# Expert weights built from one-hot products in the rounded format, with the weight's rounded part and rest side by side

## The chip, the cores and the metric

The kernel runs on one core of a Trainium2 chip. The time is device microseconds of one execution. TensorE is called PE in the views (its weight loads PEld), VectorE is DVE, ScalarE is ACT, GpSimd is POOL and SyncE, which here only starts transfers, is SP.

## What is computed

Two transformer-like blocks are applied to 256 tokens of width 2048. The change is in the last part, the feed-forward layer with 16384 single-neuron experts. Each token scores two sets of 128 keys per head, takes the best 16 pairs for each of 8 heads, and so selects 128 experts, each with a softmax weight:

```python
eidx = jnp.take_along_axis(cidx, tp, axis=-1)
gw = jax.nn.softmax(tv, axis=-1).astype(h.dtype)
...
a = jnp.einsum('td,ted->te', xc, expert_u[ic])
a = jax.nn.gelu(a, approximate=False) * wc
return jnp.einsum('te,ted->td', a, expert_v[ic])
```

The kernel does not gather experts. It computes all 16384 activations for all tokens (the "u" products), multiplies them by a dense table of weights that is zero where a token did not select the expert, and multiplies the result by all of `expert_v` (the "v" products). All arithmetic is float32, and the outputs are float32.

## The kernel before, in words

Weight matrices stream from memory as tiles `raw` of 128x2048. Each half of a tile (128x1024) is split in two parts in the rounded float32 format (`F32R` in the code, fp32r in the rows): ACT copies it to `whi` (rounded part), DVE subtracts to get `wlo` (rest). Three products per piece (rounded x rounded, rounded x rest, rest x rounded) stand for one float32 product. PE consumes one half after the other. Every half costs ACT one `whi` copy and DVE one `wlo` subtraction, and up to three halves are prepared ahead (`LOOK`).

The last part, `peer`, runs the list `PEER_ORDER`: u products for the groups 0 to 12, then v products for the groups 0 to 3, and so on. A u half is 16 products `pu` on PE. After every fourth half one result leaves PSUM: ACT copies its second part (`pul`), DVE adds the first (`raw_a<-pu,pul`), ACT applies Gelu. Group g of v needs `weigh` first: the activations times the dense weights (read back from memory as `wrd`), split again into `As`.

The dense weights are made by `expert_weights` and `weight_products` while PE works on u. For a token, the table of 128x128 weights is a sum over its 128 selections: one-hot of the second key, times one-hot of the first key times the weight. That is one product of two 128x128 matrices per token. Four tokens are one step of the loop, called a quad here. There are 64 quads. Before, a quad takes DVE one `is_equal` over 128x512 and four `tensor_scalar` (compare and multiply by the weight in one instruction), PE four float32 products `pw` of 128 columns, and ACT four copies into the staging tiles `wst`. Eight quads are written to memory (`wd`) by four transfers on SP. `weigh` waits for all 64 quads.

The order of instructions on each engine is fixed when the program is built. Work is written as threads (generators); a planner keeps an estimated clock for each engine and takes the next piece of a thread when that engine would be free. `yield "a"`, `"d"` and `"p1"` hand the next piece to ACT, DVE and PE; `ring` is the set of one-hot buffers that may be in flight. On the chip every engine then runs its list strictly in that order and waits where an operand is not there. Almost every row of the views has the line L408, the helper through which all instructions pass, so the tiles' names tell the rows apart.

Of the kernel before, what the change touches and what calls it, by code (L numbers as in the profile page):

```python
# [10 lines left out]
F32 = mybir.dt.float32  # L11
F32R = mybir.dt.float32r
I32 = mybir.dt.int32
U32 = mybir.dt.uint32
AF = mybir.ActivationFunctionType
ALU = mybir.AluOpType
# [155 lines left out]
PEER_ORDER = (("u", 0, 13), ("v", 0, 4), ("v", 4, 8), ("v", 8, 12), ("u", 13, 20), ("v", 12, 18), ("u", 20, 26), ("v", 18, 24),  # L172
              ("u", 26, 32), ("v", 24, 32))
SPARE = 2
RING = 4
LAG = 2
GATE_AT = 120
EV_ORDER = (1, 2, 5, 6, 3, 7, 8, 9, 10)
# [256 lines left out]
class K:  # L435
# [1705 lines left out]
    def expert_weights(self, tk, sel):  # L2141

        nc = self.nc
        yield from self.after(tk)
        cols = self.ar("selT", F32, (128, 3, 256))
        for w in range(3):
            yield "p1"
            pt = self.ms("selp", (128, 256))
            for tt in range(2):
                self.tr(pt[:, tt * 128:(tt + 1) * 128], sel[:, w, tt, :], self.cst("ident"))  # L2150
            yield "a"
            nc.scalar.activation(cols[:, w, :], pt, AF.Copy)
        yield "d"
        io = self.cst("iota")

        ring = [self.ar("oneh", F32, (128, 2, 4, 128)) for _ in range(RING)]
        made, used = [], []
        out = self.add(self.weight_products(ring, made, used), 4)
        for i in range(64):
            while i - len(used) >= RING:  # L2160
                yield "w"
            yield "d", 0.0
            o, t = ring[i % RING], 4 * i
            nc.vector.tensor_tensor(o[:, 0], io[:, None, :].to_broadcast([128, 4, 128]), cols[:, 1, t:t + 4, None].to_broadcast([128, 4, 128]),
                                    op=ALU.is_equal)
            for j in range(4):
                nc.vector.tensor_scalar(o[:, 1, j, :], io, cols[:, 0, t + j:t + j + 1], cols[:, 2, t + j:t + j + 1],
                                        op0=ALU.is_equal, op1=ALU.mult)
            made.append(self.clock.t["dve"])
        yield from self.after([out])  # L2170

    def weight_products(self, ring, made, used):
        nc = self.nc
        for i in range(64):
            if i % 8 == 0:
                st = [self.ar("wst", F32, (128, 32, 32)) for _ in range(4)]
            while len(made) <= i:
                yield "w"
            yield "p1", made[i]
            o = ring[i % RING]  # L2180
            pw = self.ms("pw", (128, 4, 128))
            for j in range(4):
                self.mm(pw[:, j, :], o[:, 0, j, :], o[:, 1, j, :], start=(j == 0), stop=True, skip_group_check=True)
            used.append(i)
            yield "a"
            for q in range(4):
                nc.scalar.activation(st[q][:, :, 4 * (i % 8):4 * (i % 8) + 4], pw[:, :, 32 * q:32 * q + 32].rearrange("p t i -> p i t"), AF.Copy)
            if i % 8 == 7:
                for q in range(4):
                    nc.sync.dma_start(self.wd[i // 8][:, 32 * q:32 * q + 32, :], st[q])  # L2190
# [83 lines left out]
```

## Time and profile before

| | |
|---|---|
| median of 3 runs | 3181.95 us (3176.02 to 3182.89) |
| profiled execution, its time | 3181.01 us |
| its span, first to last instruction | 3179.2 us |
| PE busy, share of the span | 3109.9 us, 98% |
| DVE busy | 2269.5 us, 71% |
| ACT busy | 1491.6 us, 47% |
| mean granted TensorE clock | 0.991 of full speed |

A busy share is an average over the whole program. The change touches only the stretch in which the expert weights are made, from about 1793 us on, so the share of each engine has to be read in that stretch.

### The profile page before, as it was taken

To read this page: it belongs to the slowest core of one execution; us is meant where nothing else is said; L and a number is where in the kernel's file an instruction comes from. 1 tells how busy PE (TensorE), PEld (TensorE's weight loads), DVE (VectorE), ACT (ScalarE), POOL (GpSimd) and SP (SyncE) were. 2 spreads that over 40 slices of the span, in tenths; PEclk is the share of its full clock that TensorE was granted. 3 is DMA by queue.
4 is the path that set the end of the run, shared out by engine and by line. 5 is a ranking of instruction groups with operands and counts; after the bars stand their busy time and mean duration, and the time that the engine had idled before them with its cause. 6 is when DMAs were issued, how large, how long until landed. Compare 5 with 4: busy or idle time off the path is not lost.

```text
span 3179.2 us, 48367 instructions
## 1 busy us (share of the span) xinstructions
PE 3109.9 (98%) x19516; PEld 2695.7 (85%) x19516; DVE 2269.5 (71%) x3455; ACT 1491.6 (47%) x2033; POOL 13.3 (0%) x26
## 2 busy tenths in 40 slices
PE   6899999999999999999999999999999999999999
PEld 5676899789997778999998898888888888888887
DVE  4499789777788886768689997555566656555654
ACT  3335554444445556544354565444444445434433
POOL 0000000000000000000000000000000000000000
PEclk8999999999999999999999999999999999999999
DMA  8877686888785655677655567666566666656663
GB/s 328 336 266 264 237 330 225 311 299 301 284 316 199 226 212 175 248 265 279 252 185 173 186 226 253 203 215 209 201 230 234 242 223 239 240 212 205 232 211 133
DMA packets 140944, 763.44 MB, mean 240 GB/s; under 512 B 12640, under 2 KB 45408, under 8 KB 54064
## 3 DMA queue, kind: packets, MB, share of 16 engines
q1 hardware_dynamic: 137680, 750.83, 66.3%
q0 software_dynamic: 1888, 6.37, 0.6%
q8 instruction: 153, 2.51, 0.3%
q10 hardware_dynamic: 1152, 3.15, 0.3%
q14 instruction: 71, 0.58, 0.0%
HBM read 739.33 MB, written 20.97 MB: 239 GB/s over the span
## 4 chain that ended last, share of the span: by engine, by line
PE 89%; DVE 7%; ACT 2%; DMA 1%; issue 1%; SPq 0%; ACTq 0%; DVEq 0%
PE ps L408 26%; PE pv L408 25%; PE pu L408 20%; PE q L408 6%; PE adaps L408 3%; DVE wlo L408 2%; PE pw L408 2%; PE last L408 1%; PE S L408 1%; PE kvc L408 1%; PE kv L408 1%; DMA raw<-in_ada_dram 1%; DVE si L408 1%; PE po L408 1%; PE bu L408 0%
## 5 line engine op out<-in xcount | busy, mean ns | idle before, releaser
L408 DVE TENSOR_TENSOR wlo<-raw,whi 128x1024 fp32r<-128x1024 f32 x970 | 1176.9, 1220 | 579.8 <-PE pv L408 264.3
L408 ACT ACTIVATE whi<-raw 128x1024 fp32r<-128x1024 f32 x970 | 1021.7, 1059 | 1131.3 <-PE pv L408 389.4
L408 PE MATMUL pu<-hs,whi 128*128 128x512 f32 x2048 | 726.9, 399 | 0.0
L408 PE MATMUL ps<-hs,whi 128*128 128x256 f32 x3712 | 695.3, 289 | 25.0 <-ACT hs L408 16.5
L408 PEld LDWEIGHTS ps<-hs,whi 128*128 128x128 f32 x3712 | 588.9, 195 | 59.7 <-issue 25.6
L408 PE MATMUL pv<-whi,As 128*128 128x512 f32 x2048 | 633.7, 390 | 0.8 <-DVE y L408 0.8
L408 PE MATMUL pu<-hs,wlo 128*128 128x256 f32 x2048 | 575.0, 281 | 1.2 <-DVE wlo L408 1.2
L408 PE MATMUL ps<-hs,wlo 128*128 128x256 f32 x1856 | 531.3, 286 | 1.5 <-DVE wlo L408 1.5
L408 PEld LDWEIGHTS pu<-hs,whi 128*128 128x128 f32 x2048 | 384.8, 188 | 92.8
L408 PEld LDWEIGHTS pv<-whi,As 128*128 128x128 f32 x2048 | 384.4, 188 | 81.7 <-DVE y L408 1.2
L408 PE MATMUL pv<-wlo,As 128*128 128x512 f32 x1024 | 398.4, 389 | 0.0
L408 PEld LDWEIGHTS pu<-hs,wlo 128*128 128x128 f32 x2048 | 386.8, 189 | 2.8 <-DVE wlo L408 2.7
L408 PEld LDWEIGHTS ps<-hs,wlo 128*128 128x128 f32 x1856 | 362.0, 195 | 2.3 <-DVE wlo L408 2.3
L408 DVE SCALAR_TENSOR_TENSOR adaacc<-raw,silc,adaacc 128x1024 f32<-128x1024 f32 x178 | 223.8, 1280 | 96.9 <-DMA raw<-in_ada_dram 96.6
L408 PEld LDWEIGHTS pv<-wlo,As 128*128 128x128 f32 x1024 | 192.2, 188 | 40.9 <-issue 1.0
L408 PE MATMUL q<-whi,hs 128*128 128x512 f32 x512 | 167.2, 397 | 0.0
L408 PE MATMUL ps<-mixs,whi 128*128 128x256 f32 x832 | 152.8, 286 | 2.1 <-ACT mixs L408 1.7
L408 PEld LDWEIGHTS ps<-mixs,whi 128*128 128x128 f32 x832 | 130.9, 193 | 5.0 <-issue 2.5
L408 PEld LDWEIGHTS q<-whi,hs 128*128 128x128 f32 x512 | 96.1, 188 | 36.1 <-issue 10.0
L408 PE MATMUL ps<-mixs,wlo 128*128 128x256 f32 x416 | 118.6, 285 | 1.6 <-DVE wlo L408 1.6
L408 PE MATMUL q<-wlo,hs 128*128 128x512 f32 x256 | 99.8, 390 | 0.0
L408 DVE SCALAR_TENSOR_TENSOR cacc<-ypad,pk,cacc 128x256 f32<-128x256 f32 x240 | 99.2, 477 | 0.0
(373 smaller groups left out, 3069.3 us busy)
## 6 DMA issues: line engine op xcount, KB each, us to landing
raw<-in_ada_dram SPq DMA_DIRECT2D x160, 1024.0 KB, 5.5
raw<-in_pu_dram SPq DMA_DIRECT2D x128, 1024.0 KB, 5.0
raw<-in_pv_dram SPq DMA_DIRECT2D x128, 1024.0 KB, 4.9
raw<-in_w_dram SPq DMA_DIRECT2D x60, 1024.0 KB, 5.0
raw<-in_od_dram SPq DMA_DIRECT2D x48, 1024.0 KB, 6.5
raw<-in_ev_dram SPq DMA_DIRECT2D x44, 1024.0 KB, 5.8
raw<-in_ada0s_dram SPq DMA_DIRECT2D x32, 1024.0 KB, 8.1
raw<-in_evo_dram SPq DMA_DIRECT2D x16, 1024.0 KB, 6.3
```

The source lines that it names most:

```text
L408: r = f(*args, **kw)
```

## The change

A quad's one-hots become one `is_equal` over 128x1024 on DVE, for both keys, in the rounded format. The multiplication by the weight moves from DVE to ACT: the weight is split once into rounded part and rest (`cols[:, 3]`, `cols[:, 2]`), and for each token ACT writes the first key's one-hot twice, scaled by the one and by the other, side by side in `onew`. PE then does one product of 256 columns per token in the rounded format in place of one float32 product of 128 columns. On the way out ACT copies the rest's half out of PSUM (`pwl`, twice per quad), and DVE adds the two halves into `wst`, in eight small additions per quad. The ring shrinks from four buffers to two pairs.

```diff
-RING = 4
+RING = 2
...
+        nc.scalar.activation(cols[:, 3, :].bitcast(F32R), cols[:, 2, :], AF.Copy)
+        nc.vector.tensor_sub(cols[:, 2, :], cols[:, 2, :], cols[:, 3, :])
+        ring = [(self.ar("oneh", F32R, (128, 2, 4, 128)), self.ar("onew", F32R, (128, 4, 2, 128))) for _ in range(RING)]
...
-            nc.vector.tensor_tensor(o[:, 0], io[:, None, :].to_broadcast([128, 4, 128]), cols[:, 1, t:t + 4, None].to_broadcast([128, 4, 128]),
+            nc.vector.tensor_tensor(o, io[:, None, None, :].to_broadcast([128, 2, 4, 128]), cols[:, 0:2, t:t + 4, None].to_broadcast([128, 2, 4, 128]),
                                     op=ALU.is_equal)
+            yield "a"
             for j in range(4):
-                nc.vector.tensor_scalar(o[:, 1, j, :], io, cols[:, 0, t + j:t + j + 1], cols[:, 2, t + j:t + j + 1],
-                                        op0=ALU.is_equal, op1=ALU.mult)
-            made.append(self.clock.t["dve"])
+                for z in range(2):
+                    nc.scalar.activation(ow[:, j, z, :], o[:, 0, j, :].bitcast(F32), AF.Copy, scale=cols[:, 3 - z, t + j:t + j + 1])
+            made.append(self.clock.t["act"])
...
-            pw = self.ms("pw", (128, 4, 128))
-            for j in range(4):
-                self.mm(pw[:, j, :], o[:, 0, j, :], o[:, 1, j, :], start=(j == 0), stop=True, skip_group_check=True)
-            used.append(i)
-            yield "a"
-            for q in range(4):
-                nc.scalar.activation(st[q][:, :, 4 * (i % 8):4 * (i % 8) + 4], pw[:, :, 32 * q:32 * q + 32].rearrange("p t i -> p i t"), AF.Copy)
+            for z in range(2):
+                yield "p1", made[i]
+                o, ow = ring[i % RING]
+                pw = self.ms("pw", (128, 2, 2, 128))
+                for j in range(2):
+                    self.mm(pw[:, j], o[:, 1, 2 * z + j, :], ow[:, 2 * z + j], start=(j == 0), stop=True, skip_group_check=True)
+                if z == 1:
+                    used.append(i)
+                yield "a"
+                lo = rest[:, 2 * (i % 2) + z]
+                nc.scalar.activation(lo, pw[:, :, 1, :], AF.Copy)
+                yield "d"
+                c = 4 * (i % 8) + 2 * z
+                for q in range(4):
+                    s = slice(32 * q, 32 * q + 32)
+                    nc.vector.tensor_add(st[q][:, :, c:c + 2], pw[:, :, 0, s].rearrange("p t i -> p i t"), lo[:, :, s].rearrange("p t i -> p i t"))
```

Three places of the order show how the planner places this. The first is ACT's list in the stretch of the u products. Before, from the first quads on:

```order
L408 ACTIVATE whi<-raw 128x1024
L408 ACTIVATE pul<-pu 128x512
L408 ACTIVATE wst<-pw 128x32x4 x4
L408 ACTIVATE raw_a<-raw_a 128x512
L408 ACTIVATE wst<-pw 128x32x4 x4
L408 ACTIVATE whi<-raw 128x1024
L408 ACTIVATE wst<-pw 128x32x4 x8
L408 ACTIVATE whi<-raw 128x1024
```

And the same place of ACT's list now (`onew` are the scaled one-hots, `pwl` the rest's half of the product):

```order
L408 ACTIVATE onew<-oneh,selT 128x128 x8
L408 ACTIVATE pwl<-pw 128x256 x2
L408 ACTIVATE onew<-oneh,selT 128x128 x8
L408 ACTIVATE whi<-raw 128x1024
L408 ACTIVATE pul<-pu 128x512
L408 ACTIVATE pwl<-pw 128x256
L408 ACTIVATE onew<-oneh,selT 128x128 x8
L408 ACTIVATE whi<-raw 128x1024
L408 ACTIVATE raw_a<-raw_a 128x512
L408 ACTIVATE pwl<-pw 128x256 x3
L408 ACTIVATE whi<-raw 128x1024 x2
```

These eleven rows are three quads and four halves, and they repeat. Before, four copies per quad stood between the `whi` copies, about two quads to a half; now it is ten instructions per quad and three quads to four halves.

The second place is PE's list where the weights' products end. Before, after the last of them (36 more halves of u, 576 products, follow before the v products):

```order
L408 MATMUL pu<-hs,whi 128x512
L408 MATMUL pu<-hs,wlo 128x256
L408 MATMUL pw<-oneh 128x128 x8
L408 MATMUL pu<-hs,whi 128x512
L408 MATMUL pu<-hs,wlo 128x256
```

Now:

```order
L408 MATMUL pu<-hs,whi 128x512
L408 MATMUL pu<-hs,wlo 128x256
L408 MATMUL pw<-onew,oneh 128x256 x60
L408 MATMUL pv<-whi,As 128x512
L408 MATMUL pv<-wlo,As 128x512
```

60 of the 256 products, the last 15 quads, have moved behind the last u product, with nothing between them and the first v product, which needs `As`.

The third place is DVE's list where the last quads are made. Before:

```order
L408 TENSOR_TENSOR oneh<-sc,selT 128x512
L408 TENSOR_SCALAR oneh<-sc,selT 128x128 x4
L408 TENSOR_TENSOR wlo<-raw,whi 128x1024 x2
L408 TENSOR_TENSOR raw_a<-pu,pul 128x512
L408 TENSOR_TENSOR wlo<-raw,whi 128x1024 x4
L408 TENSOR_TENSOR raw_a<-pu,pul 128x512
L408 TENSOR_TENSOR raw_a<-raw_a,wrd 128x1024
L408 TENSOR_TENSOR wlo<-raw,whi 128x1024
L408 TENSOR_TENSOR As<-raw_a,As 128x2x256 x2
```

And now, beside those 15 quads (`wst` are the additions):

```order
L408 TENSOR_TENSOR wst<-pw,pwl 128x32x2 x20
L408 TENSOR_TENSOR oneh<-sc,selT 128x1024 x2
L408 TENSOR_TENSOR wst<-pw,pwl 128x32x2 x4
L408 TENSOR_TENSOR oneh<-sc,selT 128x1024
L408 TENSOR_TENSOR wst<-pw,pwl 128x32x2 x20
L408 TENSOR_TENSOR raw_a<-raw_a,wrd 128x1024
L408 TENSOR_TENSOR As<-raw_a,As 128x2x256 x2
```

The second to the fifth of these rows come four times, once for every three quads: the last additions of three quads stand ahead of the next quad's one-hots. Before, `wlo` and u results filled DVE between the last one-hots and the first use of `wrd`; now there is nothing between the last additions and that use.

## Rows read from the trace of the kernel before

**Rows 1.** Chain that ended last, 1700 to 2100 us: start, length, what

```profile
1796.37 2.78 PE pu L408 x16
1799.15 1.78 PE pw L408 x16
...
1941.94 101.76 PE pu L408 x576
2043.70 56.45 PE pv L408 x249
```

**Rows 2.** Window of 50 us: length, PE, PEld, DVE, ACT, POOL busy, PEclk, DMA

```profile
1850.00:1900.00 50.00, 50.00 (x351) 46.18 (x350) 49.85 (x123) 30.69 (x105) 0.00 (x0) 1.00 0.67 250
```

**Rows 3.** Groups by form, 1790 to 1950 us: busy us, mean ns, idle before

```profile
L408 DVE TENSOR_SCALAR oneh<-sc,selT 128x128 f32<-128x128 f32 x256 | 71.0, 339 | 1.3 <-ACT selT L408 1.3
L408 PE MATMUL pw<-oneh 128*128 128x128 f32 x512 | 62.4, 275 | 0.0
...
L408 ACT ACTIVATE wst<-pw 128x128 f32<-128x128 f32 x256 | 50.3, 284 | 56.2 <-PE pw L408 52.8
...
L408 DVE TENSOR_TENSOR oneh<-sc,selT 128x512 f32<-128x512 f32 x64 | 43.6, 682 | 0.0
...
L408 ACT ACTIVATE pul<-pu 128x512 f32<-128x512 f32 x9 | 5.6, 622 | 0.0
```

**Rows 4.** Timeline of PE in an earlier layer, 256-column products in the rounded format

```profile
900.04 0.28 PE L408 MATMUL ps<-mixs,wlo 128*128 128x256 f32 x1
900.16 0.40 PE L408 MATMUL ps<-mixs,whi 128*128 128x256 f32 x2
```

**Rows 5.** Groups by form, whole span, ACT with a scale operand and from PSUM

```profile
L408 ACT ACTIVATE P<-P,sm 128x256 f32<-128x256 f32 x8 | 4.0, 496 | 0.0
...
L408 ACT ACTIVATE P<-P,sm 128x128 f32<-128x128 f32 x8 | 3.2, 398 | 2.4 <-DVE sm L408 2.4
...
L408 ACT ACTIVATE selT<-selp 128x256 f32<-128x256 f32 x3 | 1.1, 376 | 1.5 <-PE selp L408 1.5
```

**Rows 6.** Timeline of ACT: start, length of the merged instructions

```profile
893.65 1.69 ACT L408 ACTIVATE sq<-x,pk 128x256 f32<-128x256 f32 x4
1227.57 0.81 ACT L408 ACTIVATE P<-P,sm 128x128 f32<-128x128 f32 x2
1958.88 1.99 ACT L408 ACTIVATE whi<-raw 128x1024 fp32r<-128x1024 f32 x2
```

**Rows 7.** Groups by form, whole span, DVE

```profile
L408 DVE TENSOR_TENSOR eq<-abf,sc 128x1024 f32<-128x1024 f32 x8 | 9.7, 1217 | 0.0
...
L408 DVE TENSOR_TENSOR cand<-sv 128x64 f32<-128x64 f32 x4 | 0.9, 220 | 0.0
...
L408 DVE TENSOR_TENSOR mod<-adapt,pk 128x16 f32<-128x16 f32 x9 | 1.5, 171 | 6.9 <-PE adapt L408 6.8
```

**Rows 8.** Timeline of DVE where the first quad is made

```profile
1793.12 1.11 DVE L408 TENSOR_SCALAR oneh<-sc,selT 128x128 f32<-128x128 f32 x4 [1.27 <-ACT selT L408]
```

**Rows 9.** Timeline of ACT, then DVE, from the last quad to the first `As`

```profile
1941.09 1.68 ACT L408 ACTIVATE wst<-pw 128x128 f32<-128x128 f32 x8 [1.94 <-PE pw L408]
...
1956.56 1.23 DVE L408 TENSOR_TENSOR raw_a<-raw_a,wrd 128x1024 f32<-128x1024 f32 x1 [1.08 <-DMA wrd<-wd]
1957.70 1.22 DVE L408 TENSOR_TENSOR wlo<-raw,whi 128x1024 fp32r<-128x1024 f32 x1
1958.83 1.29 DVE L408 TENSOR_TENSOR As<-raw_a,As 128x512 fp32r<-128x512 f32 x2
```

**Rows 10.** Windows at the program's start (columns as in rows 2)

```profile
30.00:35.00 5.00, 3.92 (x18) 3.72 (x19) 4.63 (x7) 5.00 (x6) 0.00 (x0) 0.59 1.03 425
...
50.00:60.00 10.00, 6.72 (x66) 4.29 (x58) 4.63 (x12) 3.40 (x5) 0.00 (x0) 0.91 0.90 342
```

**Rows 11.** Timeline of PE in the first of these windows

```profile
31.96 0.63 PE L408 MATMUL ps<-hs,whi 128*128 128x256 f32 x2
...
32.60 0.63 PE L408 MATMUL ps<-hs,whi 128*128 128x256 f32 x2
```

More of the change, by code (lines that the diff above doesn't have):

```diff
@@ L2144, in expert_weights @@
         yield from self.after(tk)
-        cols = self.ar("selT", F32, (128, 3, 256))
+        cols = self.ar("selT", F32, (128, 4, 256))
         for w in range(3):
@@ L2154, in expert_weights @@
         io = self.cst("iota")
-        ring = [self.ar("oneh", F32, (128, 2, 4, 128)) for _ in range(RING)]
+        nc.scalar.activation(cols[:, 3, :].bitcast(F32R), cols[:, 2, :], AF.Copy)
+        nc.vector.tensor_sub(cols[:, 2, :], cols[:, 2, :], cols[:, 3, :])
+        ring = [(self.ar("oneh", F32R, (128, 2, 4, 128)), self.ar("onew", F32R, (128, 4, 2, 128))) for _ in range(RING)]
         made, used = [], []
@@ L2162, in expert_weights @@
             yield "d", 0.0
-            o, t = ring[i % RING], 4 * i
-            nc.vector.tensor_tensor(o[:, 0], io[:, None, :].to_broadcast([128, 4, 128]), cols[:, 1, t:t + 4, None].to_broadcast([128, 4, 128]),
+            (o, ow), t = ring[i % RING], 4 * i
+            nc.vector.tensor_tensor(o, io[:, None, None, :].to_broadcast([128, 2, 4, 128]), cols[:, 0:2, t:t + 4, None].to_broadcast([128, 2, 4, 128]),
                                     op=ALU.is_equal)
+            yield "a"
             for j in range(4):
-                nc.vector.tensor_scalar(o[:, 1, j, :], io, cols[:, 0, t + j:t + j + 1], cols[:, 2, t + j:t + j + 1],
-                                        op0=ALU.is_equal, op1=ALU.mult)
-            made.append(self.clock.t["dve"])
+                for z in range(2):
+                    nc.scalar.activation(ow[:, j, z, :], o[:, 0, j, :].bitcast(F32), AF.Copy, scale=cols[:, 3 - z, t + j:t + j + 1])
+            made.append(self.clock.t["act"])
         yield from self.after([out])
@@ L2173, in weight_products @@
         nc = self.nc
+        rest = self.ar("pwl", F32, (128, 4, 2, 128))
         for i in range(64):
@@ L2178, in weight_products @@
                 yield "w"
-            yield "p1", made[i]
-            o = ring[i % RING]
-            pw = self.ms("pw", (128, 4, 128))
-            for j in range(4):
-                self.mm(pw[:, j, :], o[:, 0, j, :], o[:, 1, j, :], start=(j == 0), stop=True, skip_group_check=True)
-            used.append(i)
-            yield "a"
-            for q in range(4):
-                nc.scalar.activation(st[q][:, :, 4 * (i % 8):4 * (i % 8) + 4], pw[:, :, 32 * q:32 * q + 32].rearrange("p t i -> p i t"), AF.Copy)
+            for z in range(2):
[14 more added lines that the diff above has]
+                    nc.vector.tensor_add(st[q][:, :, c:c + 2], pw[:, :, 0, s].rearrange("p t i -> p i t"), lo[:, :, s].rearrange("p t i -> p i t"))
             if i % 8 == 7:
```

## The prediction

> **What bounds the kernel now.** The chain that ended last comes first. In the stretch of the expert weights it is PE without a gap: a u half of 2.78 us, then two quads of weights' products in 1.78 us, 0.89 a quad, and so on [rows 1]. After the last quad 576 u products (36 halves, 101.8 us) run before the first v product at 2043.7 us [rows 1]. So PE sets the end, and what follows the last quad (transfer, multiplication, split) has a hundred microseconds of cover. The busy times of that stretch come next: in 50 us PE 50.0, DVE 49.85, ACT 30.7 [rows 2]. DVE has nothing left over either, but the chain does not run through it: the planner only filled it. ACT has 19 us of idle time in 50, of which the views put 52.8 us in all on waiting for the products [rows 3].
>
> **The change part by part.** *PE.* Removed: 64 quads of 0.89 us, 57.0 us [rows 1]. Added: 256 products of 256 columns in the rounded format, 0.12 us each from start to start [rows 4], 30.7 us. If nothing else happened, 26.3 us would be gained.
>
> *DVE, per quad.* Removed: 71.0 + 43.6 us over 64 quads, 1.79 us [rows 3]. Added: one comparison of 128x1024, 1.22 us alone [rows 7], and 1.13 from start to start, as its kind shows at 1956.56, 1957.70 and 1958.83 [rows 9]. So instructions in a row overlap by about 0.085 us. Eight additions of 128x64: the nearest row is 0.220 us [rows 7], less that overlap 0.135. Bounds: 0.135, and 0.30 if the pieces of two elements that they write cost double. I take 0.135: the row of 128x16 that reads PSUM with gaps lasts 0.171 us [rows 7], what the slope between the rows of 1024 and 64 elements (1.04 ns per element) gives without any penalty. A quad is then 1.13 + 1.08 = 2.2 us.
>
> *ACT, per quad.* Removed: four copies, 50.3 us over 64 quads, 0.79 us [rows 3]. Added: two copies of 256 columns out of PSUM, 0.376 us alone [rows 5], 0.29 in a row, and eight scaled copies of 128 columns. An unscaled copy of 128 columns takes 0.284 us and eight in a row 1.68 [rows 3, 9], so 0.20 from start to start. With a scale per partition one takes 0.398 us [rows 5]. How much of that overlaps decides. Two of them in a row took 0.81 us [rows 6], no overlap: 0.40 is the upper bound, 0.20 the lower. Four of 256 columns in a row, also with a scale, took 1.69 us [rows 6] where one takes 0.496 [rows 5]: 0.40 from start to start, an overlap of 0.10. I take 0.398 - 0.10 = 0.30, since a run of four says more of a run of eight than a pair whose second may have waited for its operand. A quad is 8 x 0.30 + 2 x 0.29 = 3.0 us, nearly four times what it was.
> The Trainium skill (ScalarE: Activation LUTs, What ACT_TABLE_LOAD costs) gives 186 ns plus 0.833 ns per column, about 93 more for each pointer operand, and an overlap of about 93 back to back. An estimate from that page is 293 ns per scaled copy, and by it the total below would be 3.5 us lower. The same page (Rules for kernel authors) sends plain multiplications to VectorE, not ScalarE, against what this change does; the 0.339 us of one scaled one-hot on DVE [rows 3] beside 0.398 on ACT agrees.
>
> *The stretch beside u.* ACT's rows of the order repeat after three quads and four halves. ACT: 24 x 0.30 = 7.2, six PSUM copies 1.7, four `whi` at 0.95 (two take 1.99 [rows 6]) 3.8, one `pul` and one Gelu at about 0.53 each [rows 3] 1.05. That is 13.75 us. PE: 4 x 2.8 + 12 x 0.12 = 12.6. DVE: three comparisons and four `wlo` at 1.13, one result 0.6, 24 x 0.135 = 11.75. ACT is the longest, where before it had room. It also waits: after a quad's last scaled copy the two copies out of PSUM behind it need that quad's first product, and behind those stand the next `whi`, for which PE waits later. I count 0.5 us for one such place and 0.4 for another in the period (two products, and a half that PE still has to finish). So 14.65 us per period. In the first 49 quads there are 16 periods: 234.4 us.
> When does it begin? Before, the first scaled one-hots started when the weights' last column arrived, at 1793.1 us [rows 8]. Now there follow the copy and subtraction that split the weight (0.3 + 0.4), one `wlo` and the comparison on DVE (1.14 + 1.2), and eight scaled copies (2.5): quad 0 is ready at 1798.7 us, quad 48 at 2033.1.
>
> *The end.* 15 quads now stand behind the last u product, and PE, which has nothing else, waits for each. The rest of ACT's list up to the one-hots of quad 52 adds to 15.3 us: three more quads of scaled copies 7.2, eight PSUM copies 2.3, two `whi`, a `pul` and a Gelu 2.95, waits for products 0.8, then additions and a comparison on DVE, 2.05. Then four rounds of three quads. A round is 9.0 us on ACT (24 x 0.30 + 6 x 0.29), three waits for the products 1.35, and the turn that the order shows: the last additions (0.65 with the first one's full length), the comparison behind them (1.22) and two hand-offs (0.2), while ACT has nothing. 12.4 us, four times, less the last comparison 1.3: 48.3 us. Together 63.6.
> Then the trip through memory, which had cover before: from the last copy into `wst` (1941.09 + 1.68) to the first use of the weights read back, 1956.56, 13.8 us [rows 9], and 3.0 more to the first `As` (its first half ends at 1958.83 + 0.68, a 128x512 subtraction being as long as the comparison of that size [rows 3]) [rows 9]. The queue on SP holds nothing new ahead of it. First v product: 2033.1 + 63.6 + 16.8 = 2113.5 us instead of 2043.7, 69.8 later.
> *Restart.* PE will have done little for 60 us. At the program's start, after idle time, the granted clock was 0.59 in one window [rows 10], that is for the most part the level of 1.2 GHz, and three products of 256 columns took 0.64 us [rows 11] instead of 0.36. Six microseconds like that cost about 3. From there on the order is that of before.
>
> Sum: 69.8 + 3 = 72.8 us on the profiled execution's 3181.01 us (which lies 0.9 us under the median of the three runs): **3254 us**.
>
> **The rivals.**
> (a) *Scaled copies do not overlap*, 0.40 us each, as the pair shows. +2.4 us in 16 periods and +0.8 in each of 15 quads, 50 us: 3304 us.
> (b) *They take 0.20 us*, as unscaled ones. ACT's period falls to 12.2 and PE's 12.6 with half a microsecond of waits decides: 16 x 1.55 + 12 = 37 us less, 3217 us.
> (c) *The additions become the bound.* At 0.30 us DVE has 15.7 us a period, 16.6 with waits, and each turn is 0.65 longer: 16 x 2.0 + 2.6 = 35 more, 3289 us. Against it stands the row with gaps in PSUM; nothing here shows two-element pieces in SBUF. The Trainium skill (SBUF — State Buffer, section on the DMA port swizzle) says that accesses that leave a 16-byte line pay. By that rule it goes this way; no run so far shows it on DVE.
> (d) *PE's clock drops beside u as well*, because PE is busy 12.6 of 14.65 us there. At 0.64/0.36 a period is 22.4 us on PE, 16 x 7.75 = 124 more: 3378 us. Against it: with PE busy 67% of a window at the start the clock was 0.91 [rows 10], and 86% is more. The Trainium skill (TensorE: Matmul & The Clock Gate, HAM oscillation) has gaps between bursts of products throttle the clock; by that rule, if it acts on PE's 2.05 us of waits per period, the sum is this one.
> (e) *Faster: the 26.3 us arrive.* PE at its own pace would end u at 2043.7 - 57.0 + 49 x 0.48 = 2010.2 us. For no loss the 15 quads behind it must be done in 33.5 - 16.8 = 16.7 us, 1.1 us each; that is the point from which it decides. Did the end cost nothing at all, the time would be 3155 us. DVE alone needs 2.2 us a quad, so I give it almost nothing.
>
> **How the numbers follow.** My forecast 0.62 (its own range 3235 to 3275), (a) 0.13, (b) 0.08, (c) 0.10, (d) 0.04, (e) 0.03. For the range I go up into (a) and down into (b): 3215 to 3302 leaves out (d), (e), about half of (a) and half of (b), some 0.18. A difference of 0.2%, 6 us, is what a measurement of this kernel can tell from none. Slower than that: all but (e), 0.96; the same 0.02; faster 0.02.
>
> **What would show it.** PE: products `pw` as 256 of 256 columns, about 0.12 us apart where two stand in a row, and idle time of some 60 to 80 us right before the first v product, released by ACT's scaled copies, then by the transfer and `As`. In the stretch beside u: ACT busy over 90%, PE below 90%, waiting for `onew`. Scaled copies at 0.30 us from start to start, additions at 0.135. A lower granted clock only at the end. I am wrong if PE is still full beside u, if the wait ahead of v is below 40 us, or if DVE and not ACT is what PE waits for.

## The result, and the profile after

| | before | after |
|---|---|---|
| median | 3181.01 us (3176.02 to 3182.89, 4 runs) | 3269.49 us (3268.09 to 3275.30, 4 runs) |
| profiled execution, its span | 3181.01, 3179.2 us | 3275.30, 3273.5 us |
| first v product | 2043.70 us [rows 1] | 2135.88 us |

The changed kernel takes 1.0289 times as long, 95% interval 1.0273 to 1.0304: slower, by 88.5 us between the medians and 94.3 us between the profiled executions. The loss is complete when v starts: 92.2 us later.

The first view is the table by windows of the changed kernel. After the length of the window come the busy times of PE, PEld, DVE, ACT and POOL, the granted clock, and DMA; the row of before that answers is [rows 2].

```profile
1850.00:1900.00 50.00, 46.24 (x243) 37.65 (x242) 37.98 (x102) 44.04 (x117) 0.00 (x0) 0.97 0.50 172
...
2060.00:2080.00 20.00, 10.07 (x31) 5.78 (x29) 14.01 (x41) 14.32 (x44) 0.00 (x0) 0.62 0.42 158
2080.00:2100.00 20.00, 12.60 (x22) 6.14 (x22) 9.77 (x39) 15.59 (x54) 0.00 (x0) 0.50 0.24 95
2100.00:2130.00 30.00, 13.94 (x24) 6.89 (x24) 15.43 (x67) 17.69 (x60) 0.00 (x0) 0.50 0.20 74
```

Beside u PE no longer fills its time (46 of 50 us, before 50). ACT is the busiest of the preparing engines at 44, DVE has fallen from 49.85 to 38. But ACT is not full either: **no engine is**, which already says that some of the time is a wait of one engine for another. From 2062 us on u has nothing left, PE does 22 to 24 products in 20 or 30 us, and its clock is at 0.50, the level of 1.2 GHz.

Next the groups of equal instructions from 1785 to 2150 us: busy us, mean ns of one, and the idle time of the engine before them with what ended it (its releaser). They answer to [rows 3].

```profile
L408 ACT ACTIVATE onew<-oneh,selT 128x128 fp32r<-128x128 f32 x512 | 156.3, 391 | 39.3 <-DVE oneh L408 39.3
...
L408 PE MATMUL pw<-onew,oneh 128*128 128x256 f32 x256 | 84.4, 380 | 48.2 <-ACT onew L408 47.7
L408 DVE TENSOR_TENSOR oneh<-sc,selT 128x1024 fp32r<-128x1024 f32 x64 | 77.2, 1213 | 0.0
L408 DVE TENSOR_TENSOR wst<-pw,pwl 128x64 f32<-128x64 f32 x512 | 76.6, 215 | 75.1 <-ACT pwl L408 60.4 <-DMA wd<-wst 14.4
...
L408 ACT ACTIVATE pwl<-pw 128x256 f32<-128x256 f32 x128 | 43.5, 372 | 6.0 <-PE pw L408 5.5
```

Read the releasers as a circle. PE waits for ACT's scaled copies (`onew`, 47.7 us), ACT's scaled copies wait for DVE's comparison (`oneh`, 39.3), and DVE's additions, which stand ahead of the comparison in its list, wait for ACT's copies of the rests (`pwl`, 60.4). Before, the only large wait of the kind was ACT's for the products, 52.8 us [rows 3], and ACT had the time.

One turn of that circle beside u, first in the chain that ended last (start, length, what), then in the timelines of DVE and ACT:

```profile
1858.20 2.45 ACT onew L408 x8
...
1865.54 2.35 ACT onew L408 x8
...
1867.93 0.39 PE pw L408
1868.32 2.21 PE pu L408 x13
1870.53 0.26 DVE wst L408 x2
1870.80 1.13 DVE wlo L408
1871.92 0.53 DVE wst L408 x4
1872.45 1.14 DVE oneh L408
...
1873.68 1.57 ACT onew L408 x5
```

```profile
1869.65 1.14 DVE L408 TENSOR_TENSOR wst<-pw,pwl 128x64 f32<-128x64 f32 x8 [2.00 <-ACT pwl L408]
...
1867.78 1.06 ACT L408 ACTIVATE whi<-raw 128x1024 fp32r<-128x1024 f32 x1
1868.72 0.63 ACT L408 ACTIVATE raw_a<-raw_a 128x512 f32<-128x512 f32 x1
1869.25 0.91 ACT L408 ACTIVATE pwl<-pw 128x256 f32<-128x256 f32 x3
1870.04 2.08 ACT L408 ACTIVATE whi<-raw 128x1024 fp32r<-128x1024 f32 x2
1873.68 1.57 ACT L408 ACTIVATE onew<-oneh,selT 128x128 fp32r<-128x128 f32 x5 [1.56 <-DVE oneh L408]
```

DVE waits 2.00 us, since ACT has a `whi` and a Gelu (`raw_a<-raw_a`) ahead of `pwl`. Then DVE does additions, a `wlo`, additions and the comparison, 4 us, in which ACT runs out of work after its two `whi` and waits 1.56 us. From 1858.20 to 1873.68 is one period of three quads.

The end, in the chain from 2000 us on:

```profile
2012.16 8.90 DMA wd<-wst
...
2060.21 4.38 DMA wd<-wst
...
2095.97 4.45 DMA wd<-wst
...
2103.48 1.97 ACT onew L408 x7
...
2111.71 1.66 DVE wst L408 x12
2113.37 1.14 DVE oneh L408
...
2114.54 1.97 ACT onew L408 x7
...
2122.76 1.54 DVE wst L408 x11
...
2127.09 6.83 DMA wrd<-wd
...
2135.88 14.26 PE pv L408 x53
```

A round of three quads takes 11.06 us (2103.48 to 2114.54), and in it the turn from the last `pwl` over additions and comparison to the next copies is as forecast. New are three places where the chain goes through the transfer of the finished weights: the first additions of a new group of eight quads write staging tiles that got the slots of the group before, which a transfer is still reading.

### The profile page after: what moved, and what is told of

Same layout as the page of the kernel before. It is cut to its first block, busy times and chain, and to the rows that moved or that the text cites. A ratio compares the mean times of both kernels' runs of the same rounds, so it can differ in the third digit from the quotient of the medians.

```text
span 3273.5 us, 48533 instructions
## 1 busy us (share of the span) xinstructions
PE 3145.4 (96%) x19260; PEld 2694.6 (82%) x19260; DVE 2307.5 (70%) x3712; ACT 1627.1 (50%) x2418; POOL 13.2 (0%) x26
## 4 chain that ended last, share of the span: by engine, by line
PE 82%; DVE 9%; ACT 6%; DMA 2%; issue 1%; SPq 0%; ACTq 0%; DVEq 0%
PE ps L408 26%; PE pv L408 24%; PE pu L408 17%; PE q L408 5%; ACT onew L408 3%; PE adaps L408 3%; DVE wlo L408 3%; PE last L408 1%; DVE oneh L408 1%; PE kvc L408 1%; DVE wst L408 1%; PE S L408 1%; PE kv L408 1%; DMA raw<-in_ada_dram 1%; ACT whi L408 1%
## 5 line engine op out<-in xcount | busy, mean ns | idle before, releaser
L408 ACT ACTIVATE onew<-oneh,selT 128x128 fp32r<-128x128 f32 x512 | 156.3, 391 | 39.3 <-DVE oneh L408 39.3
L408 PE MATMUL pw<-onew,oneh 128*128 128x256 f32 x256 | 84.4, 380 | 48.2 <-ACT onew L408 47.7
L408 DVE TENSOR_TENSOR wst<-pw,pwl 128x64 f32<-128x64 f32 x512 | 76.6, 215 | 75.1 <-ACT pwl L408 60.4
```

The source lines that it names most:

```text
L408: r = f(*args, **kw)
```

## The experiments

Each kernel is the changed one with the edit shown, unless the text says otherwise. Before was run beside each on the same chip: 3177.35 us for e1 to e4, medians 3177.14 for e5 to e8 and 3179.05 for e9 to e11. The changed kernel was not run beside them, its time is the 3269.49 us of the result. e6 is the median of 11 runs and e11 of 6, the others are one run each; single runs of before lay between 3173.49 and 3187.92 us, so a difference of a few us between two single runs tells nothing.

**e1: half of the scaled copies left out.**

```diff
...
-                for z in range(2):
-                    nc.scalar.activation(ow[:, j, z, :], o[:, 0, j, :].bitcast(F32), AF.Copy, scale=cols[:, 3 - z, t + j:t + j + 1])
+                nc.scalar.activation(ow[:, j, 0, :], o[:, 0, j, :].bitcast(F32), AF.Copy, scale=cols[:, 3, t + j:t + j + 1])
...
```

> Leaves out the rest's scaled copies: that half of the scaled one-hots is written once with zeros, so ACT has 4 scaled copies per quad instead of 8 (the weights lose their rest). The order of all other instructions is unchanged, 15 quads still stand behind the last u product. Theory (ACT's scaled copies set the pace): a period of three quads and four halves beside u falls from 15.75 us to what PE and DVE need with waits, 13 to 13.5, 16 x 2.3 = 37 us, and each of the 15 quads at the end loses 4 x 0.294 = 1.18 us, 18 us: about 3215 us, 3205 to 3230. Rival (the hand-offs ACT to DVE and back, and the staging tiles, set the pace, the copies only fill the time between): less than 20 us come off, 3250 or more.

Measured: 3217.34 us. Its window beside u, one behind it, and its first v product in the chain:

```profile
1850.00:1900.00 50.00, 50.00 (x299) 44.16 (x298) 44.80 (x120) 40.12 (x89) 0.00 (x0) 1.00 0.60 205
...
2040.00:2060.00 20.00, 8.76 (x24) 6.91 (x24) 13.02 (x54) 10.72 (x35) 0.00 (x0) 0.50 0.27 107
```

```profile
2078.35 71.75 PE pv L408 x309
```

With 1.2 us less per quad on ACT, PE is full beside u from 1800 to 1950 us and its clock at 1.00: the side-by-side products, the copies out and the additions are hidden there. From 1950 to 2000 us it is busy for 45.67 us. Most of what is left of the loss stands behind u, where the last quads and the trip have no cover.

**e2: the last sixteen quads left out.**

```diff
-        for i in range(64):
+        for i in range(48):
...
```

The loop of the products is cut in the same way, and the rows of `wd` that stay free are written from tiles of other quads.

> Leaves out the last 16 of 64 quads; the transfers of the last two groups of eight send the two groups before once more. Nothing stands behind the last u product any more. Theory (the quads behind u cost their full time): quad 47 is in the staging tile near 2060 us, the trip through memory and the split take 11 more, so v starts near 2071 us instead of 2136: 65 us less, about 3205 us, 3195 to 3215, still some 24 above before with a quarter of the work gone, because beside u PE waits. Rival (the end is lost anyway, by clock or transfers): above 3235.

Measured: 3224.88 us, v from 2084.46 us, between the two theories' numbers. The timelines of DVE and SP at its end show where some of it comes from:

```profile
2063.12 0.62 DVE L408 TENSOR_TENSOR wst<-pw,pwl 128x64 f32<-128x64 f32 x4 [1.55 <-ACT pwl L408]
2063.37 8.20 SPq L408 DMA_DIRECT2D wd<-wst  x8
...
2072.90 9.41 SPq L408 DMA_DIRECT2D wrd<-wd  x4
```

Last additions to first v product took 20.7 us here and 11.6 in the changed kernel. The edit doubled the transfers at the end (8.20 us on SP's queue, 2.86 in the changed kernel); behind them stand a transfer of `raw` and a slower read-back, which the edit may or may not have caused. Take all 9 us off and 3216 is left, just above what the theory had. The run bears the theory out only with that correction, which was worked out and not run.

**e3: added up in PSUM, without DVE.** Eight products of 128 columns that accumulate, four copies out by ACT:

```diff
...
+            for j in range(4):
+                for z in range(2):
+                    self.mm(pw[:, j, :], o[:, 1, j, :], ow[:, j, z, :], start=(j == 0 and z == 0), stop=(z == 1), skip_group_check=True)
+            for q in range(4):
+                nc.scalar.activation(st[q][:, :, 4 * (i % 8):4 * (i % 8) + 4], pw[:, :, 32 * q:32 * q + 32].rearrange("p t i -> p i t"), AF.Copy)
...
```

> Computes the whole result. Rounded part and rest are no longer side by side: per token two products of 128 columns add up in PSUM, and ACT copies the sum out in four copies per quad as before the change; DVE adds nothing. The planner then ends the products some 25 halves ahead of the first v product. Theory (ACT is the bound): ACT needs 8 x 0.294 + 0.8 = 3.15 us a quad, more than the 2.9 of the change, and 202 + 45 x 1.2 = 256 us beside 45 halves, so the products end near 2055 us, then 25 halves: v starts near 2125, about 3258 us, 3245 to 3270. Rival (DVE's additions and the end behind u set the time): with both gone the time falls to 3215 or below. What a product of 128 columns costs in the rounded format is open: 0.06 us if only columns count, 0.12 if it costs as much as 256.

Measured: 3239.11 us, under the theory's 3245 and far above the rival.

```profile
1850.00:1900.00 50.00, 48.31 (x241) 40.28 (x241) 27.34 (x24) 50.00 (x176) 0.00 (x0) 0.86 0.48 170
```

Without the circle through DVE's additions ACT is full, 50.00 of 50 us, and alone sets the pace; DVE now waits for the products. PE looks busy, but at a clock of 0.86 and with fewer instructions than before (241 against 351 [rows 2]). So the additions are not the whole loss: without them 61.8 of the 88.5 us remain, and ACT's list, in which the scaled copies are the largest part, is enough for those.

**e4: the planner told what a scaled copy costs.**

```diff
+        if hasattr(kw.get("scale"), "tensor") and x.shape[-1] == 128 and out.dtype == F32R:
+            cost = 0.294
```

> Same work as the change, only the planner's price of a scaled copy is raised from its 0.146 us to the 0.294 us measured. The planner then leaves 31 quads behind the last u product instead of 15. Theory (the work itself is too much for the place): beside u 33 quads let PE run at nearly its own pace, u ends near 2005 us, and 31 quads at 3.7 us and the trip of 13 follow: v starts near 2132, about 3265 us, 3250 to 3280, no better. Rival (the time is lost because the planner had the wrong price and interleaved badly): clearly faster, below 3240.

Measured: 3273.36 us.

```profile
1850.00:1900.00 50.00, 50.00 (x295) 43.91 (x294) 39.59 (x94) 44.77 (x108) 0.00 (x0) 1.00 0.62 216
...
2040.00:2060.00 20.00, 12.06 (x21) 5.89 (x21) 12.30 (x52) 15.57 (x54) 0.00 (x0) 0.50 0.00 0
```

With the right price PE is full beside u, and 31 quads stand uncovered behind it instead of 15. The order only moves the wait: ACT and DVE have the same work to do before v can start.

**e5 and e9: without the transfers of the first seven groups.** In e5 their rows are written once, early, from another tile; e9 leaves that out too and reads the last group's rows for all:

```diff
-        nc.sync.dma_start(w, self.wd[:, :, 4 * g:4 * g + 4, :].rearrange("b p i t -> p b i t"))
+        nc.sync.dma_start(w, self.wd[7, :, None, 4 * g:4 * g + 4, :].to_broadcast([128, 8, 4, 32]))
...
-            if i % 8 == 7:
+            if i == 63:
```

> The changed kernel without the transfers of the finished weights of the first seven groups of eight quads (their rows of the DRAM array are written once, early, from another tile, so the weights that follow are not the right ones; order of all engines unchanged, the last group's transfers stay). The chain of the changed kernel holds 17.7 us of the transfer wd<-wst (8.90, 4.38 and 4.45) ahead of the first additions of a new group, since the staging tiles come back to slots that a transfer still reads. Theory (these waits are the part of the time that the forecast did not have): 17.7 us go, 3253, between 3245 and 3262. Rival (other work ends only little earlier, and the scalar engine's scaled copies take up the time): at least 3266.

> e5 again without its early transfers: the transfers of the finished weights of the first seven groups are left out, and the weights are read back from the last group's rows for all groups, so the weights that multiply u are not the right ones; as many bytes are read back, and the order of all engines' instructions is that of the changed kernel but for the transfers left out. In e5 the early transfers from another tile pushed the first quad from 1798.7 to 1814.5, and from the first quad's copies to the first product of v it took 324.1 us, against 337.2 in the changed kernel. Theory (the waits of a new group's first additions for the transfer of the group before lie on the path): 13 to 18 us go: 3257, between 3251 and 3263. Rival (they are taken up by other waits): 3268 or more.

Measured: 3277.97 and 3271.24 us. Both times are the rival's. The waits from the first copies to v in e9 (us in all, times, longest); in the changed kernel they were 60.4 and 39.3 us, and 14.4 of DVE for the transfer, which is gone here:

```profile
DVE wst L408 <- ACT pwl L408: 62.4, 41, 2.9
...
ACT onew L408 <- DVE oneh L408: 31.6, 23, 2.4
```

From the first scaled copy to the first v product the stretch is 324.1 us in e5 and 326.2 in e9, against 337.2, so 11 to 13 us shorter and not 17.7. Of that, e5 lost 15.8 us before its first quad, through its own early transfers. e9 began 2.7 us later and took 4.1 us more after v had started; in that stretch its chain goes through read-backs of the weights (`wrd`) that the changed kernel's chain does not have, and PE is busy for 1.7 us less from 2150 to 3260 us, which is part of the 4.1. The rest has no one cause in the rows. My theory, that the chain's 17.7 us would come back, falls: in the total e9 is 4 us under the profiled execution and nothing under the median, no more than runs differ.

**e6: the scaled one-hots shared out.** On e3: four of eight by DVE in one instruction each, the key comparison only where it is used, a ring of three, and the price of e4:

```diff
...
+            for j in range(2):
+                for z in range(2):
+                    nc.vector.tensor_scalar(ow[:, j, z, :], io, cols[:, 0, t + j:t + j + 1], cols[:, 3 - z, t + j:t + j + 1],
+                                            op0=ALU.is_equal, op1=ALU.mult)
...
```

> All of the computation is kept. As in e3, a quad's eight products of 128 columns accumulate rounded part and rest in PSUM, and the scalar engine copies four pieces out. New: of the eight scaled one-hots of a quad, four are made by the vector engine from iota in one instruction each (compare and multiply), four by the scalar engine, the key comparison is made only where it is used, and the ring has three places. e3's profile: eight products in 1.00 us (before 1.78), eight scaled copies in 2.34, four copies out in 0.84, conversion 1.05; the page of before has 0.257 start to start for compare and multiply. For three quads beside two halves of u: tensor engine 3 x 1.00 + 2 x 2.78 = 8.6 us, scalar engine 3 x (1.18 + 0.84) + 2.1 = 8.2, vector engine 3 x 1.95 + 2.4 = 8.3. Theory (what the changed kernel loses is the scalar engine's and the additions' work, not the rounded products): the tensor engine sets the time, 64 x 0.78 = 50 us less than before, some 10 us of waits back: 3137, between 3122 and 3160. Rival (chains between three engines at over 0.95 of their time wait as much as in e3, and the tensor engine's clock falls): 3200 or more.

Measured: 3179.05 us, 1.0003 of before (0.9991 to 1.0015, 11 runs).

```profile
1850.00:1900.00 50.00, 50.00 (x336) 45.51 (x335) 50.00 (x121) 46.92 (x163) 0.00 (x0) 1.00 0.60 213
```

The expectation rests on a slip of mine: 1.78 us is two quads in the kernel before, not one [rows 1]: each of its 256 float32 products stands as two records [rows 3]. With 0.89 for a quad, eight accumulating products at 0.105 to 0.125 us (0.84 to 1.00 in all) gain next to nothing on PE, and no change is what the engines' sums say. The useful half of the theory holds: with the work shared out PE waits nowhere, even with DVE at 50.00 and ACT at 47 of 50 us, so the losses of the changed kernel and of e3 are the preparing engines' and not the format's.

**e7 and e8:** two places in the ring, with two (e7) or four (e8) of the eight scaled one-hots on DVE.

> As e6, with two places in the ring, and two of the eight scaled one-hots of a quad by the vector engine, six by the scalar engine. Five quads beside four halves: scalar engine 5 x (1.76 + 0.84) + 4.2 = 17.2 us, tensor engine 5 x 1.00 + 4 x 2.78 = 16.1, vector engine 5 x 1.57 + 4.9 = 12.7. Theory: the scalar engine sets the time by 1.1 us of each five quads, 13 in all, and waits come on top: 30 us above e6, between 3140 and 3185. Rival (waits of the ring and not the scalar engine's sum): like e3, over 3220.

> As e6 with two places in the ring in place of three (the buffers that the changed kernel has). Theory (the engines' sums set the time): within 15 us of e6. Rival (the turn vector engine, scalar engine, tensor engine through two places sets it): 40 us or more above e6.

Measured: 3182.19 and 3187.67 us, PE at 50.00 of 50 us in each window of 50 us beside u from 1800 to 2000. e8 is 8.6 us above e6, within its theory: with DVE free of additions, two places do not set the time. Whether more places would open the circle in the changed kernel itself was not run. e7's forecast (30 us above e6) fails, it is 3 above; both lie inside the runs of e6 (3175.71 to 3188.18). e7's ACT is at 49.2 to 49.9 of 50 us without costing PE anything beside u, since more of u stands beside the quads (96 u products are left behind the last one, 384 in e6).

**e10: a shorter comparison, in the same order.**

```diff
...
-            nc.vector.tensor_tensor(o, io[:, None, None, :].to_broadcast([128, 2, 4, 128]), cols[:, 0:2, t:t + 4, None].to_broadcast([128, 2, 4, 128]),
+            nc.vector.tensor_tensor(o[:, :, 0:1], io[:, None, None, :].to_broadcast([128, 2, 1, 128]), cols[:, 0:2, t:t + 1, None].to_broadcast([128, 2, 1, 128]),
...
```

> The changed kernel with a key comparison over 256 elements in place of 1024 (only the first of a quad's four; the other three keep the one-hots that are made once ahead of the quads, so the weights are not the right ones); the planner is charged as before, and the order of every engine is the same. e6's profile: 407 ns for 256 elements against 1213 for 1024, 0.8 us less for each of 64. The vector engine is busy 38 of 50 us beside u, the scalar engine 44. Theory (the scalar engine waits for the turn from copied-out rests over additions and comparison to the next scaled copies, once in three quads beside u, once in two or three behind it): 16 x 0.8 and 5 x 0.8, 16 us less: 3257, between 3250 and 3264. Rival (the scalar engine's own sum sets the time, and its waits for the comparison are filled from elsewhere): 3268 or more.

Measured: 3251.87 us, 17.6 us less than the changed kernel's median. Chain beside u (L2169 is the comparison's line in this kernel):

```profile
1850.75 2.46 ACT onew L408 x8
...
1864.99 0.34 DVE oneh L2169
...
1865.42 2.46 ACT onew L408 x8
```

DVE was at 38 of 50 us, so by sums alone 0.8 us less per quad on it is worth nothing. Over the first six regular periods the mean fell from 15.71 us (1810.94 to 1905.18) to 14.73 (1806.43 to 1894.78), and the stretch from first copy to v from 337.2 to 316.9. Of the 1.0 us per period 0.8 are the comparison's: periods with a granted clock of 1.00 all through took 15.47 to 15.76 us in the changed kernel and 14.67 to 14.96 in e10. The rest is PE's clock, which e10 kept at 1.00 in all six and the changed kernel did not in two of them (0.89). That shows that the circle sets the time beside u, and that DVE's comparison is a link of it.

**e11: rounded one-hots and nothing else.** An edit of the kernel before:

```diff
-        ring = [self.ar("oneh", F32, (128, 2, 4, 128)) for _ in range(RING)]
+        ring = [self.ar("oneh", F32R, (128, 2, 4, 128)) for _ in range(RING)]
```

> The kernel before with its one-hots in the rounded format and nothing else: four products of 128 columns a quad, the weight rounded and its rest left out of the computation. No additions on the way out, no scaled copies by the scalar engine. e6's profile gives 0.125 us for such a product, 0.50 a quad; the kernel before takes 1.78 for two quads, 0.89 a quad (in e6's expectation this was wrongly taken as one quad's). 64 x 0.39 = 25 us less work for the tensor engine. The vector engine, at 49.85 of 50 us before, has 64 x 1.7 + 47 x 1.4 = 175 us of work while the quads last, the tensor engine 64 x 0.50 + 47 x 2.78 = 163, so up to 12 us of waits. Theory (the rounded products gain their time wherever the preparing engines keep up): 3158, between 3147 and 3168. Rival (the vector engine, being full before, gives nothing away): 3172 or more.

Measured: 3152.25 us, 0.9919 of before (0.9900 to 0.9937): 26.8 us faster.

```profile
1850.00:1900.00 50.00, 50.00 (x312) 44.66 (x311) 50.00 (x115) 32.79 (x103) 0.00 (x0) 1.00 0.71 256
```

```profile
2015.92 184.09 PE pv L408 x812
```

v starts 27.8 us earlier than before [rows 1]. PE stays full although DVE is too. The gain of the format on PE is real. With the weight's rest it is gone in e6, and in the changed kernel the rest, as it is made there, costs more than the format gives.

## Why the prediction was right, and where it was too low

The side and the mechanism were right: ACT becomes the longest engine beside u, PE waits for `onew`, 15 quads and the trip stand uncovered behind u. Three of the signs I named came out otherwise beside u: from 1850 to 1900 us ACT was busy 88% of the time, not over 90, and PE 92%, not below 90; and the clock fell there too and not only at the end. None of the signs of being wrong came. The size was too low by 15.5 us against the median and 21.5 against the profiled execution. Term by term, on the latter:

| term | forecast | measured |
|---|---|---|
| scaled copy, start to start | 0.30 us | 0.294 (eight in 2.45, the last 0.39) |
| rest copied out, in a row | 0.29 | 0.27 |
| addition | 0.135 | 0.132 (eight in 1.14, the last 0.215) |
| comparison, in a row | 1.13 | 1.14 |
| quad 0 ready | 1798.7 | 1801.1 |
| 16 periods | 234.4 | 257.1 |
| from quad 48 to the last additions | 63.6 | 66.1 |
| trip through memory, to v | 16.8 | 11.6 |
| v starts later by | 69.8 | 92.2 |
| restart (measured: what is left of 94.3) | 3 | 2.1 |

*The durations* were all within 0.02 us. Rivals (a) and (b), which rested on other prices of a scaled copy, are refuted by the 0.294. The estimate of 293 ns from the Trainium skill (ScalarE: Activation LUTs, What ACT_TABLE_LOAD costs) agrees with it. Rival (c) is refuted by the 0.132 us of an addition. The rule of the Trainium skill (SBUF — State Buffer, section on the DMA port swizzle) on accesses that leave a 16-byte line is not seen here on DVE: pieces of two elements cost what contiguous rows cost (0.215 us alone, 0.220 [rows 7]).

*The step that was too small* is the stretch beside u, and in it the waits: "0.5 us for one such place and 0.4 for another". Starts of periods, and a half of u, in the chain that ended last:

```profile
1810.94 2.45 ACT onew L408 x8
...
1826.41 2.46 ACT onew L408 x8
...
1829.30 4.34 PE pu L408 x16
...
1842.44 2.46 ACT onew L408 x8
...
1965.81 2.46 ACT onew L408 x8
...
1980.77 2.46 ACT onew L408 x8
```

The six periods from 1810.94 to 1905.18 us took 15.71 us on average, where I had 14.65. ACT's own work of 13.75 was right (busy 13.7 to 13.9 us in each), so the waits are 2.0 and not 0.9. They are also other waits. I had counted those of ACT for PE's products, and of these the whole stretch shows 5.5 us ahead of `pwl` and 3.3 ahead of `whi`, against 39.3 for DVE's comparison. I had counted the turn over additions and comparison for the end only; it happens beside u too, once a period, since DVE's list puts additions and a conversion ahead of the comparison. e10 shows it: 0.8 us off the comparison took 0.8 us off the periods with a full clock, while DVE was idle a quarter of the time.

The 22.7 us of the table are not spread evenly. The six periods make 6.3 of them, and 2.5 came ahead of the first. From 1905.18 to 1950.23 us the order of ACT's list changes, and eight quads lost 6.0; the parts of that were not taken apart. The next twelve quads lost only 1.9, three of their periods being 14.96 us. The last eight lost 6.0, with the first transfer wait of 8.90 among them.

*The transfer waits* were not in the forecast at all: I took the staging tiles for free because they had been before. The chain shows 17.7 us of them, 13.3 ahead of the four last rounds. e5 and e9 put their worth in the stretch from first copy to v at 11 to 13 us; how much of the total would return stays open.

*The end* came out near (+2.5 us) by luck, since two errors nearly cancel: a round of three quads is 11.06 us and not 12.4, which the transfer waits of 4.38 and 4.45 us made up. In a round ACT's 9.0 us and the turn of 2.1 were right, and the waits of 1.35 for the products did not come. *The trip* was 5.2 us shorter than the one of before, from which I had taken it. Until the weights are read back it took 9.6 us instead of 13.8 (2124.30 to 2133.94). What made the transfers of before slower was not tried. From there to the first v product it took 1.9 instead of 3.0, because that product waits only for ACT's `As`, where I had counted up to DVE's [rows 9]. First the product, then ACT's `As` in the kernel before, which began 1.3 us after the first use of the weights there, as it does here:

```profile
2135.88 0.79 PE L408 MATMUL pv<-whi,As 128*128 128x512 f32 x1 [12.79 <-ACT As L408]
```

```profile
1957.82 1.16 ACT L408 ACTIVATE As<-raw_a 128x512 fp32r<-128x512 f32 x2 [1.67 <-DVE raw_a L408]
```

*Rival (d)*, the clock, happened in part. Between 1829 and 1834 us the granted clock was 0.66, most of it the level of 1.2 GHz, right after 3 us in which PE was busy for 1.85; a half of u then took 4.34 instead of 2.8 us.

```profile
1829.00:1834.00 5.00, 5.00 (x21) 4.33 (x22) 3.96 (x11) 4.36 (x13) 0.00 (x0) 0.66 0.44 182
```

The rule of the Trainium skill (TensorE: Matmul & The Clock Gate, HAM oscillation) is borne out in kind. In amount it is far from the rival's 124 us: over 50 us the clock was 0.97, and of the six periods the two with such a half took 16.0 us, the others 15.5 to 15.8. *Rival (e)* is refuted: the 26 us are there on PE (e11, without the rest, has 26.8 in the time), but 15 quads behind u cost 66 us, not 17.

## What to carry to other kernels

Two engines that hand work to each other in both directions, each in a fixed order, can both have time left and still set the pace. So add up the links of the circle, not only each engine's work. Before moving work off a full engine, ask where its price is lowest: here one instruction of DVE made a scaled one-hot in 0.34 us, and its replacement took two scaled copies, half a copy out and two additions. And if a cheaper format needs a correction term, time the format alone first (e11), since it is the correction that decides.

## What had not been expected of the hardware

Where PE is full, a product in the rounded format mostly cost 0.098 to 0.107 us from start to start for 128 columns (four in 0.39 us in e11, 24 in 2.57 in e6), up to 0.125 in places, and 0.12 for 256 columns (four in 0.47). Half the columns gained little, which is why adding up in PSUM could not pay on PE.
